# Subtract, square and sum over rows: coarser pieces for the last rows, and ScalarE as the engine that waits for the store

## The chip, the cores and the metric

The kernel runs on one core of a Trainium2 chip. The metric is the device time of one execution in microseconds (us). The engines that matter here are VectorE (DVE in the profile), ScalarE (ACT), and SyncE (SP), which issues every DMA. TensorE does nothing, and GpSimd (POOL) only sets a few constants at the start.

## The reference

```python
"x": np.random.randn(1024, 4096).astype(np.float32)
"y": np.random.randn(1024, 4096).astype(np.float32)
"axis": -1
...
return np.sum((x - y) ** 2, axis=axis).astype(np.float32)
```

Two matrices of 16.8 MB each are read once; 1024 sums of 4096 squared differences come out.

## The kernel before

**Layout.** Each of the 128 partitions holds 8 consecutive rows of the matrix, so that x and y are views of 128 partitions by 32768 columns (`N`), in which row r of a partition takes the columns 4096 r to 4096 r + 4095 (L56 to L62). The on-chip buffers X and Y have room for 24576 columns (`H`, six rows) each; a column c lies at c modulo H, so the columns of rows 6 and 7 go where those of rows 0 and 1 were (`home`, L98).

**Loads.** The lists `xw` and `yw` (L72, L73) cut the columns into loads: x in 7, y in 8 and two more. Those two are `last` (the last 192 columns of row 7) and `late` (the last 128 columns of row 3, which are held back and loaded at the very end). A load of y comes after the x that it needs. Two loads (x0, y0) are put ahead of the program's opening barriers by `early` (L29), x1 and y1 follow, and they fill the buffers. The other thirteen wait on SP until ScalarE has squared row 1 (L221) and are then issued one after the other (L108). All of them go through one DMA queue, SP's, and are served in that order. In short the loads are named here by their place in the lists: x2 is the third load of x, y2 the third of y, and so on.

**Work.** The loop at L197 goes over the loads of y. VectorE waits for the load (`wait_loaded`, L164), and for each piece of it (`pieces_of`, L128: cut at the ends of rows, and, for loads 1 to 4 of y, each part cut once more in half) it subtracts Y from X in place (`sub`, L176). ScalarE waits for that subtraction and squares the piece in place (`square`, L182); an accumulator read after each square writes the sum of the piece to a column of `parts`, or straight to `results` if the row is one piece. `complete` (L187) has VectorE wait for the last square of a row and add up the row's columns (L189). After load 4 of y VectorE completes rows 4, 5 and 6; row 7 at the end. The late piece is the exception: VectorE itself squares and sums it in one instruction (L205) on top of the partial sum of row 3.

**End.** SP waits until every reduction is done, issues the store of the results (L233), clears the semaphores of the program, and waits for the store's semaphore `stored` to reach 16, from which it takes 16 off again (`close`, L40 to L45).

**Pieces of the last four rows.** Row 4 and row 5 are two pieces of 2048 columns each; row 6 is 1312, 1312, 736 and 736; row 7 is 640, 672, 672, 672, 480, 480, 288 and 192. So ScalarE makes 16 squares for the rows 4 to 7.

Of the kernel before, what the change touches and what calls it, by code (L numbers as in the profile page):

```python
# [8 lines left out]
class Program:  # L9
# [27 lines left out]
        )  # L37
        self.entry[where:where] = taken

    def close(self, engine, stored, value):  # L40

        engine.sem_clear(range(self.sems[0].num, self.sems[-1].num + 1))
        engine.wait_ge(stored, value).then_inc(stored, -value)  # L45


def kernel(tc, x, y, axis, out):
    nc = tc.nc
    P = nc.NUM_PARTITIONS  # L50
    F32 = mybir.dt.float32
    Square = mybir.ActivationFunctionType.Square
    mult, add = mybir.AluOpType.mult, mybir.AluOpType.add

    B, D = x.shape
    R = B // P  # L56
    N = R * D


    xv = x.rearrange("(p r) d -> p (r d)", p=P)  # L60
    yv = y.rearrange("(p r) d -> p (r d)", p=P)
    ov = out.rearrange("(p r) -> p r", p=P)  # L62


    H = 6 * D
    X = nc.alloc_sbuf_tensor("X", [P, H], F32).ap()
    Y = nc.alloc_sbuf_tensor("Y", [P, H], F32).ap()
    results = nc.alloc_sbuf_tensor("results", [P, R], F32).ap()

    xw = [16384, 8192, 5472, 1280, 960, 320, 160]  # L72
    yw = [16256, 8192, 2624, 2784, 1344, 480, 480, 288]  # L73
    late, last = 128, 192
    LATE = 3
    halved = (1, 2, 3, 4)
    cut = (LATE + 1) * D - late
    assert sum(xw) == N and sum(yw) == N - late - last
    xs, c = [], 0
    for w in xw:  # L80
        xs.append((c, c + w))
        c += w
    ys, c = [], 0
    for w in yw:
        ys.append((c, c + w))
        c += w
        if c == cut:
            c += late
    ys += [(N - last, N), (cut, cut + late)]

    prog = Program(nc, tc)
    stored = nc.alloc_semaphore("stored")
    diffs = prog.semaphore("diffs")
    acts = prog.semaphore("acts")
    sums = prog.semaphore("sums")
    n = dict(diffs=0, acts=0, sums=0)

    def home(c0, c1):  # L98
        h0 = c0 % H
        return slice(h0, h0 + c1 - c0)  # L100


    landed_x, landed_y = [], []
    freed = []

    def load(landed, src, dst, name, c0, c1):
        sem = prog.semaphore("%s%d" % (name, len(landed)))
        nc.sync.dma_start(out=dst[:, home(c0, c1)], in_=src[:, c0:c1]).then_inc(sem, 16)  # L108
        landed.append(((c0, c1), sem))

    order = []
    have = 0
    for c0, c1 in ys:
        while have < c1:
            order.append((landed_x, xv, X, "x") + xs[len([o for o in order if o[3] == "x"])])
            have = order[-1][5]
        order.append((landed_y, yv, Y, "y", c0, c1))

    todo = list(order)
    for _ in range(2):  # L120
        load(*todo.pop(0))
    prog.early(mybir.EngineType.SP)
    while todo and todo[0][5] <= H:
        load(*todo.pop(0))


    row_parts = [[] for _ in range(R)]
    def pieces_of(j, c0, c1):  # L128

        pieces = []  # L130
        while c0 < c1:
            e = min(c1, (c0 // D + 1) * D)
            if j in halved:
                h = (c0 + e) // 64 * 32
                pieces.append((c0, h))
                c0 = h
            pieces.append((c0, e))
            c0 = e
        return pieces

    for j, (c0, c1) in enumerate(ys):
        for piece in pieces_of(j, c0, c1):
            row_parts[piece[0] // D].append(piece)
    parts, where = None, {}
    total = sum(len(p) for p in row_parts if len(p) > 1)
    parts = nc.alloc_sbuf_tensor("parts", [P, total], F32).ap()
    k = 0
    for r, p in enumerate(row_parts):
        for piece in p:
            where[piece] = parts[:, k : k + 1] if len(p) > 1 else results[:, r : r + 1]  # L150
            k += len(p) > 1
    first = {}
    k = 0
    for r, p in enumerate(row_parts):
        if len(p) > 1:
            first[r] = k
            k += len(p)

    def parts_of(r, m):
        return parts[:, first[r] : first[r] + m]  # L160

    seen_x = [0]

    def wait_loaded(c1, ysem):  # L164

        waits = []
        while seen_x[0] < len(xs) and xs[seen_x[0]][0] < c1:
            waits.append(seen_x[0])
            seen_x[0] += 1
        nc.vector.wait_ge(ysem, 16)  # L170
        for k in waits:
            nc.vector.wait_ge(landed_x[k][1], 16)

    def sub(c0, c1):
        a = X[:, home(c0, c1)]
        nc.vector.tensor_sub(out=a, in0=a, in1=Y[:, home(c0, c1)]).then_inc(diffs, 1)  # L176
        n["diffs"] += 1

    def square(c0, c1, acc):
        a = X[:, home(c0, c1)]  # L180
        nc.scalar.wait_ge(diffs, n["diffs"])
        nc.scalar.activation(out=a, in_=a, func=Square, accum_out=acc).then_inc(acts, 1)  # L182
        n["acts"] += 1

    squared = {}

    def complete(r):  # L187
        nc.vector.wait_ge(acts, squared[row_parts[r][-1]])
        nc.vector.tensor_reduce(  # L189
            out=results[:, r : r + 1],  # L190
            in_=parts_of(r, len(row_parts[r])),
            axis=mybir.AxisListType.X,
            op=add,
        ).then_inc(sums, 1)
        n["sums"] += 1

    for j, (c0, c1) in enumerate(ys):  # L197
        final = j == len(ys) - 1
        wait_loaded(c1, landed_y[j][1])
        for piece in pieces_of(j, c0, c1):  # L200
            sub(*piece)
            r = piece[0] // D
            if final:
                nc.vector.wait_ge(diffs, n["diffs"])
                nc.vector.tensor_tensor_reduce(  # L205
                    out=Y[:, home(*piece)],
                    in0=X[:, home(*piece)],
                    in1=X[:, home(*piece)],
                    scale=1.0,
                    scalar=parts_of(r, 1),  # L210
                    op0=mult,
                    op1=add,
                    accum_out=results[:, r : r + 1],
                ).then_inc(sums, 1)
                n["sums"] += 1
                continue
            square(*piece, where[piece])
            squared[piece] = n["acts"]
            if r in (0, 1):

                nc.sync.wait_ge(acts, n["acts"])  # L221
                while todo and todo[0][5] <= H + (r + 1) * D:
                    load(*todo.pop(0))
                if r == 1:
                    while todo:
                        load(*todo.pop(0))
        if j == 4:
            for r in (4, 5, 6):
                complete(r)
    complete(7)  # L230

    nc.sync.wait_ge(sums, n["sums"])
    nc.sync.dma_start(out=ov, in_=results).then_inc(stored, 16)  # L233
    prog.close(nc.sync, stored, 16)


# [33 lines left out]
```

## Time and profile before

| what | value |
|---|---|
| time, median of 3 runs | 84.24 us (84.09 to 84.29) |
| the profiled execution: its time | 84.24 us |
| the profiled execution: its span, first to last instruction | 82.9 us |
| DVE busy | 36.9 us (44%), 27 instructions |
| ACT busy | 33.5 us (40%), 41 instructions |
| DMA queue, share of the 16 engines' span | 95.8%, 33.56 MB, mean 405 GB/s |
| subtractions (L176) | 21, 36.3 us |
| squares (L182) | 20, 31.2 us |

The span is 1.34 us shorter than the time: what lies before the first and after the last instruction isn't in the trace. A busy row of the page has one digit for each fortieth of the span, in tenths of that slice. The chain of waits lists, in order of time, what the end of the program was waiting for. In the timeline a line is a start, a length, the engine, the line of the kernel, and the tiles; in brackets is the idle time before it and what ended it. A row of the groups has the shape, the count, the busy time, the mean length in ns of one instruction, and the idle time before. A row of the DMA issues has the kilobytes and the time from the issue to the landing in us. SPq is the sequencer of SP, whose issues, waits and clears are not counted as busy.

### The profile page before, as it was taken

To read this page: it belongs to the slowest core of one execution; us is meant where nothing else is said; L and a number is where in the kernel's file an instruction comes from. 1 tells how busy PE (TensorE), PEld (TensorE's weight loads), DVE (VectorE), ACT (ScalarE), POOL (GpSimd) and SP (SyncE) were. 2 spreads that over 40 slices of the span, in tenths; PEclk is the share of its full clock that TensorE was granted. 3 is DMA by queue.
4 is the path that set the end of the run, shared out by engine and by line. 5 is a ranking of instruction groups with operands and counts; after the bars stand their busy time and mean duration, and the time that the engine had idled before them with its cause. 6 is when DMAs were issued, how large, how long until landed. Compare 5 with 4: busy or idle time off the path is not lost.

```text
span 82.9 us, 135 instructions
## 1 busy us (share of the span) xinstructions
DVE 36.9 (44%) x27; ACT 33.5 (40%) x41; POOL 0.2 (0%) x4
## 2 busy tenths in 40 slices
DVE  0000000000000000000299999999189996989992
ACT  0500000000000000000000979889886999899991
POOL 0000000000000000000000000000000000000000
DMA  9299999957999996599799979969989899999960
GB/s 506 95 411 506 506 506 506 474 221 316 502 502 502 502 502 282 220 502 502 316 443 506 427 332 506 490 269 506 411 348 496 369 405 438 430 403 421 396 214 2
DMA packets 2592, 33.56 MB, mean 405 GB/s; under 512 B 416, under 2 KB 1312, under 8 KB 1696
## 3 DMA queue, kind: packets, MB, share of 16 engines
q1 hardware_dynamic: 2592, 33.56, 95.8%
HBM read 33.55 MB, written 0.00 MB: 405 GB/s over the span
## 4 chain that ended last, share of the span: by engine, by line
DMA 64%; SPq 17%; DVE 12%; ACT 4%; issue 1%
DMA Y<-in_y_dram 64%; SPq L108 17%; DVE X L176 11%; ACT X L182 4%; DVE Y L205 0%; DVE results L189 0%; SPq L221 0%; DVE results L205 0%
## 5 line engine op out<-in xcount | busy, mean ns | idle before, releaser
L176 DVE TENSOR_TENSOR X<-X,Y 128x2048 f32<-128x2048 f32 (+10 forms) x21 | 36.3, 1779 | 44.5 <-DMA Y<-in_y_dram 44.4
L182 ACT ACTIVATE X<-X 128x2048 f32<-128x2048 f32 (+9 forms) x20 | 31.2, 1559 | 45.9 <-DVE X L176 45.8
L182 ACT ACTIVATION_READ_ACCUMULATOR X<-X 128x1 f32 x20 | 3.7, 186 | 0.0
L182 ACT ACT_TABLE_LOAD x1 | 1.3, 1283 | 1.9 <-PEq L19 1.9
L189 DVE TENSOR_REDUCE results<-parts 128x1 f32<-128x2 f32 (+2 forms) x4 | 0.4, 151 | 0.0
L205 DVE CUSTOM_DVE_ANT_0 Y<-X,parts 128x128 f32<-128x128 f32 x1 | 0.4, 353 | 0.0
L251 POOL MEMSET const-bfloat16-1.0<- 128x1 bf16 x1 | 0.1, 101 | 0.0
L251 POOL MEMSET const-uint8-127<- 128x1 uint8 x1 | 0.1, 101 | 0.0
L251 POOL MEMSET const-float32-0.0<- 128x1 f32 x1 | 0.1, 98 | 0.2 <-issue 0.2
L251 POOL MEMSET const-float32-1.0<- 128x1 f32 x1 | 0.1, 98 | 0.0
L205 DVE DVE_READ_ACCUMULATOR2_ANT results<- 128x1 f32 x1 | 0.1, 84 | 0.0
## 6 DMA issues: line engine op xcount, KB each, us to landing
Y<-in_y_dram SPq DMA_DIRECT2D x1, 8128.0 KB, 40.6
X<-in_x_dram SPq DMA_DIRECT2D x1, 4096.0 KB, 48.8
Y<-in_y_dram SPq DMA_DIRECT2D x1, 4096.0 KB, 58.2
X<-in_x_dram SPq DMA_DIRECT2D x1, 2736.0 KB, 13.4
Y<-in_y_dram SPq DMA_DIRECT2D x1, 1392.0 KB, 19.0
Y<-in_y_dram SPq DMA_DIRECT2D x1, 1312.0 KB, 16.2
Y<-in_y_dram SPq DMA_DIRECT2D x1, 672.0 KB, 21.2
X<-in_x_dram SPq DMA_DIRECT2D x1, 640.0 KB, 20.1
```

The source lines that it names most:

```text
L108: nc.sync.dma_start(out=dst[:, home(c0, c1)], in_=src[:, c0:c1]).then_inc(sem, 16)
L176: nc.vector.tensor_sub(out=a, in0=a, in1=Y[:, home(c0, c1)]).then_inc(diffs, 1)
L182: nc.scalar.activation(out=a, in_=a, func=Square, accum_out=acc).then_inc(acts, 1)
L189: nc.vector.tensor_reduce(out=results[:, r : r + 1], in_=parts_of(r, len(row_parts[r])), axis=mybir.AxisListType.X, op=add,).then_inc(sums, 1)
L205: nc.vector.tensor_tensor_reduce(out=Y[:, home(*piece)], in0=X[:, home(*piece)], in1=X[:, home(*piece)], scale=1.0, scalar=parts_of(r, 1), ...
L251: nc = _bacc.Bacc("TRN2", target_bir_lowering=False, num_devices=1)
```

## The change

Three things are edited.

- The loads after the first two are cut otherwise: x in 6, y in 7 and the two at the end, which now have 288 columns (`last`) and 160 (`late`). That makes 15 loads in place of 17. The first y load loses 32 columns, which the late piece gains.
- The halving in `pieces_of` is gone. Rows 4 and 5 are one piece each (4096), whose sums go straight to `results`; row 6 is 2656 and 1440; row 7 is 1472, 928, 896, 512 and 288. ScalarE makes 9 squares for the rows 4 to 7. Only row 6 is completed after load 4 of y.
- In `close`, ScalarE waits for the store and takes the 16 off; SP still clears the other semaphores.

```diff
-    def close(self, engine, stored, value):
+    def close(self, engine, last, stored, value):
         engine.sem_clear(range(self.sems[0].num, self.sems[-1].num + 1))
-        engine.wait_ge(stored, value).then_inc(stored, -value)
+        last.wait_ge(stored, value).then_inc(stored, -value)
...
-    xw = [16384, 8192, 5472, 1280, 960, 320, 160]
-    yw = [16256, 8192, 2624, 2784, 1344, 480, 480, 288]
-    late, last = 128, 192
+    xw = [16384, 8192, 5568, 1824, 512, 288]
+    yw = [16224, 8192, 2656, 2912, 928, 896, 512]
+    late, last = 160, 288
     LATE = 3
-    halved = (1, 2, 3, 4)
...
-    def pieces_of(j, c0, c1):
+    def pieces_of(c0, c1):
         pieces = []
         while c0 < c1:
             e = min(c1, (c0 // D + 1) * D)
-            if j in halved:
-                h = (c0 + e) // 64 * 32
-                pieces.append((c0, h))
-                c0 = h
             pieces.append((c0, e))
             c0 = e
         return pieces
...
         if j == 4:
-            for r in (4, 5, 6):
+            for r in (6,):
                 complete(r)
     complete(7)
...
-    prog.close(nc.sync, stored, 16)
+    prog.close(nc.sync, nc.scalar, stored, 16)
```

More of the change, by code (lines that the diff above doesn't have):

```diff
@@ L139, in pieces_of @@
         return pieces
-    for j, (c0, c1) in enumerate(ys):
-        for piece in pieces_of(j, c0, c1):
+    for c0, c1 in ys:
+        for piece in pieces_of(c0, c1):
             row_parts[piece[0] // D].append(piece)
@@ L199 @@
         wait_loaded(c1, landed_y[j][1])
-        for piece in pieces_of(j, c0, c1):
+        for piece in pieces_of(c0, c1):
             sub(*piece)
```

## The prediction, on record before the changed kernel ran

> **What bounds the kernel now.** I read the page first. Its busy shares (DVE 44%, ACT 40%, DMA queue 95.8%) are averages over a span of which the first 41 us only load, so the 40 slices (2.07 us each) say more.
>
> ```profile
> DVE  0000000000000000000299999999189996989992
> ACT  0500000000000000000000979889886999899991
> DMA  9299999957999996599799979969989899999960
> ```
>
> The loads run without a hole until slice 38. In the last ten slices VectorE (DVE) and ScalarE (ACT) are nearly full too: three resources run out almost together, and the end must be read from the chain of waits (start, length, what; us).
>
> ```profile
> 67.69 12.66 DMA Y<-in_y_dram
> ...
> 80.37 0.57 DVE X L176 x2
> ...
> 80.96 0.35 DVE Y L205
> 81.32 0.01 DVE results L205
> 81.33 0.11 DVE results L189
> ```
>
> The last-but-one y load lands at 80.34; VectorE then needs two subtractions (192 and 128 columns), the fused square of the late piece (L205) and the reduction of row 7 (L189). SP issues the store at 81.47. But that reduction also waits for ScalarE's last square; the timeline shows how close that is.
>
> ```profile
> 69.45 1.91 ACT L182 ACTIVATE X<-X 128x2048 f32<-128x2048 f32 x1 [0.20 <-DVE X L176]
> ...
> 71.76 1.30 ACT L182 ACTIVATE X<-X 128x1312 f32<-128x1312 f32 x1 [0.31 <-DVE X L176]
> ...
> 80.81 0.34 ACT L182 ACTIVATE X<-X 128x192 f32<-128x192 f32 x1
> ...
> 81.06 0.18 ACT L182 ACTIVATION_READ_ACCUMULATOR X<-X 128x1 f32 x1
> ...
> 81.28 0.16 DVE L189 TENSOR_REDUCE results<-parts 128x1 f32<-128x8 f32 x1
> ```
>
> ScalarE delivers at 81.06 + 0.18 = 81.24 and the reduction starts at 81.28. Other ScalarE and VectorE instructions also start 0.03 us after the one they wait for, so ScalarE has no slack: whatever delays it delays the end.
>
> **The change part by part.** Durations of other widths come from the rows by shape (busy, mean ns).
>
> ```profile
> L176 DVE TENSOR_TENSOR X<-X,Y 128x4096 f32<-128x4096 f32 x3 | 13.1, 4421 | 41.0 <-DMA Y<-in_y_dram 41.0
> L176 DVE TENSOR_TENSOR X<-X,Y 128x2048 f32<-128x2048 f32 x4 | 8.9, 2286 | 2.2 <-DMA Y<-in_y_dram 2.2
> L182 ACT ACTIVATE X<-X 128x4096 f32<-128x4096 f32 x3 | 10.8, 3617 | 43.5 <-DVE X L176 43.5
> L182 ACT ACTIVATE X<-X 128x2048 f32<-128x2048 f32 x4 | 7.6, 1910 | 1.5 <-DVE X L176 1.5
> L182 ACT ACTIVATE X<-X 128x288 f32<-128x288 f32 x1 | 0.4, 426 | 0.0
> ```
>
> A subtraction is 0.15 us + 1.04 ns a column ((4421-2286)/2048), and the next starts 0.08 before it ends. A square is 0.20 us + 0.834 ns a column; its accumulator read ends 0.09 after it, and the next square doesn't wait for that.
>
> *Loads.* Thirteen loads follow the first four; the change has eleven. A landing is issue start (timeline) plus time to landing (DMA issues): y1 at 2.29 + 58.2 = 60.5, then
>
> ```profile
> X<-in_x_dram SPq DMA_DIRECT2D x1, 2736.0 KB, 13.4
> Y<-in_y_dram SPq DMA_DIRECT2D x1, 1392.0 KB, 19.0
> Y<-in_y_dram SPq DMA_DIRECT2D x1, 1312.0 KB, 16.2
> ```
>
> 53.63 + 13.4 = 67.03 for x2, 54.00 + 16.2 = 70.2 for y2, 54.48 + 19.0 = 73.5 for y3: 1.20 ns a column. Loads of 480 columns take about 1.3 ns a column and the last small ones 1.4 to 1.5, so a load itself costs some 0.04 to 0.08 us. Two fewer save 0.1 us, and 32 columns moved from y0 to the late piece bring y1 0.04 earlier. New landings: y1 60.46, x2 (5568) 67.11, y2 (2656) 70.30, y3 (2912) 73.78, x3 (1824) 75.96, y4 (928) 77.07, y5 (896) 78.15, x4 and y6 (512 each, 0.65) 79.45, x5 and last (288 each, 0.36) 80.17, late (160) 80.39, against 80.5 before. SP's issue instructions block for 2.6 to 4.8 us each near the end, but each load still lands 9.9 us or more after its issue began, so fewer issues gain nothing more.
> The Trainium skill's page "DMA: Bandwidth & Descriptors" (Anatomy of one DMA; Rules for kernel authors) gives a DMA a fixed cost of about 2.0 us, fitted on another issuing path, and says that transfers under 64 KB pay mostly overhead. Taken as a cost in this queue, two loads fewer would save 4 us and the time would be near 80.2, an estimate by that page; but thirteen times 2.0 is 26 us, more than the 20.0 us in which all thirteen land here. The row decides.
>
> *VectorE, rows 4 to 7.* Rows 4 and 5 become one subtraction each, from 60.48 to 60.48 + 4.34 + 4.42 = 69.24. The 2656 piece waits for y2: 70.32 + 2.92 = 73.24. Then 1440 (73.80 to 75.45), 1472 (to 77.06), 928 on its landing (77.10 to 78.22), one reduction in place of three, 896 (78.21 to 79.30), 512 on its landing (79.48 to 80.17), 288 on its landing (80.20 to 80.65), 160 (80.58 to 80.89), the fused square from 80.93. Before, the reduction started 0.32 after the fused square; 32 more columns make it 0.35: VectorE is ready at 81.28, as before. The earlier landing and the longer last pieces cancel.
>
> *ScalarE, rows 5 to 7.* Here the halves are missed. Row 5's square starts at 69.27 and frees ScalarE at 72.89. The 2656 square can't start before 73.24 + 0.03 = 73.27, where the first half started at 71.76 before. From there on the squares are back to back, each subtraction ending at or before its turn (1472 just in time, the others with 0.2 to 0.4 to spare): 2656, 1440, 1472, 928, 896, 512 and 288 columns take 2.42 + 1.40 + 1.43 + 0.97 + 0.95 + 0.63 + 0.43 = 8.23. So 73.27 + 8.23 = 81.50, accumulator read to 81.59, reduction at 81.62 in place of 81.28. **+0.34 us.** The check: the start is 1.51 later, five fewer squares at 0.20 give back 1.0, and the gaps of before (0.12) go. The wait is now ScalarE's, and VectorE idles 0.34 ahead of the last reduction.
>
> *Other reductions.* Those of rows 4 and 5 vanish and row 6's has two parts. It waits for the 1440 square, done at 77.2, and VectorE gets there at 78.15: no stall. If ScalarE were a microsecond later, VectorE would stand there with 896, 512, 288 and late queued behind it.
>
> *The closing wait.* SP keeps the store's issue and the clear of the semaphores; ScalarE waits for the store. Nothing is queued behind it in the program, and ScalarE's own work ends 1.6 us before the store lands.
>
> ```profile
> SPq L45 <- SPq L45: 1.0, 1, 1.0
> ```
>
> Inside the span this is a swap: at the three barriers at the start (L251, L19; semaphore records of the trace) SP and ACT wake from one release 4 to 5 ns apart, in the second at 1.503 and 1.508, and take 17 ns each. What follows the last instruction, part of the 84.24 - 82.90 = 1.34 us around the span, isn't in the trace. From below: if all that SP does after its last instruction now runs during the store, at most the 1.0 us that it waits there can be gained. From above: an extra hand-over among the engines, at most like a whole barrier at the start (SP's release in the first at 1.176, in the second at 1.503), +0.33. I take 0, by the nearest row, the 5 ns, and keep -1.0 and +0.33.
> The Trainium skill's page "Runtime: NRT & Kernel Launch" (The ~15µs preamble/postamble breakdown) names a barrier after the kernel that waits for all engines, and for the one before it a walk of 44 ns a hop over eight hops. Which engine is last could by that page move the end by a few hops, some 0.2 us either way as an estimate; no row here shows it.
>
> **The sum**, against the profiled execution, whose time of 84.24 is also the median: 84.24 + 0.34 (ScalarE) + 0 (closing) = **84.58 us**, span 83.24. About 0.3% (0.25 us) is what a measurement of this kernel can tell from no change.
>
> **The rivals.**
> - *Forecast*: ScalarE's late start, closing free: 84.58, with 0.1 us of doubt in the landing of y2, which the whole ScalarE chain follows. Chance 0.50.
> - *Closing costs* up to a barrier: 84.6 to 84.91. For: nothing in the trace covers what follows the last instruction. Against: 5 ns at the starting barriers. 0.10.
> - *The cost is smaller, or half covered*: y2 lands early (ScalarE can't start before 72.89, so 84.20 at best), or handing the end to ScalarE gains 0.1 to 0.6: 83.99 to 84.48. For: y2's stretch has only one row of evidence. 0.27.
> - *Faster, by the closing*: SP's own exit is the long part outside the span, and it now runs beside the store's 1.0 us. It must exceed 0.34 to beat before and 0.59 to show; at its full price 84.58 - 1.0 = 83.58. For: SP is idle from 81.93 to 82.89 and still has a queue to close; its drain after the first issues takes 125 ns where ACT's takes 8. Against: that is a fifth of what is needed. 0.13.
> - *The change doesn't do what it says* (the time outside is the same whoever waits) is the forecast itself.
>
> **Numbers.** Slower by over 0.3% (above 84.49): 0.50 + 0.10, less the doubt of y2 = 0.57. Same: 0.27 and that doubt = 0.30. Faster 0.13. The range goes from 83.99, which leaves out the last rival alone, to 84.91.
>
> **What would show it.** ScalarE without a gap from 73.3 to 81.5; the chain of waits ending through a square of 288 columns instead of the late piece; the last landing near 80.4; the store issued near 81.81. A first long square near 73.0 would mean that y2 was early. Closing shows as a change of the time outside the span, 1.34 now. A store at 81.47 or earlier would make the ScalarE step wrong; a time outside the span that moved by more than 0.1 would make the closing step wrong.

## The result and the profile after

The changed kernel takes 84.75 us (median of 4 runs, 84.69 to 84.88) against 84.27 us for the kernel before in the same comparison: a ratio of 1.0064, 95% interval 1.0044 to 1.0083. It is slower by 0.54 us (0.37 to 0.70). The forecast was 84.58 us and slower; the sign, the engine and more than half of the size came as forecast, one term didn't.

The profiled execution of the changed kernel takes 84.88 us with a span of 83.38 (before: 84.24 and 82.90). So the loss of this execution lies in two places: 0.48 us more inside the span, and 1.50 us around the span in place of 1.34.

The page of the changed kernel, busy shares in 40 slices of 2.08 us:

```profile
DVE  0000000000000000000299999999099994979981
ACT  0500000000000000000001979797970797989991
DMA  9299999957999999299989979997999999999940
```

In the 34th slice (68.8 to 70.9) VectorE waits for y2 and is 4 tenths busy (6 before); from the 37th on (75.1) ScalarE is hardly ever idle, and in the 39th (79.2 to 81.3), where the loads end, ScalarE is at 9 and VectorE at 8 (both 9 before). The chain of waits of the changed kernel (start, length, what) ends through ScalarE:

```profile
54.05 16.39 DMA Y<-in_y_dram
70.45 0.02 issue
70.47 2.94 DVE X L170
73.41 0.02 issue
73.43 8.29 ACT X L176 x14
81.72 0.02 issue
81.74 0.16 DVE results L183
```

Before, the chain ran from the last loads through VectorE. Now the load named is y2, which lands at 70.45, eleven microseconds before the end; one subtraction follows, and then seven squares with their accumulator reads (x14) with no gap over 0.02 us. A second chain ends almost level with this one. The load y3 brings 1440 and 1472 columns, and the second of its two subtractions ends at 75.53 + 1.69 = 77.22; the square of those 1472 columns starts 0.03 later, at 77.25, just as ScalarE comes free:

```profile
75.53 1.69 DVE L170 TENSOR_TENSOR X<-X,Y 128x1472 f32<-128x1472 f32 x1
75.85 1.39 ACT L176 ACTIVATE X<-X 128x1440 f32<-128x1440 f32 x1
77.25 1.43 ACT L176 ACTIVATE X<-X 128x1472 f32<-128x1472 f32 x1
```

So an earlier start of ScalarE's run would by itself not end it earlier; e10 below shows that. VectorE is the one that waits at the end, as the waits of the changed kernel say (us in total, times, longest):

```profile
DVE results L183 <- ACT X L176: 0.2, 1, 0.2
```

The timeline of the changed kernel shows both engines at the end:

```profile
80.57 0.62 ACT L176 ACTIVATE X<-X 128x512 f32<-128x512 f32 x1
...
81.14 0.38 DVE L199 CUSTOM_DVE_ANT_0 Y<-X,parts 128x160 f32<-128x160 f32 x1
81.18 0.43 ACT L176 ACTIVATE X<-X 128x288 f32<-128x288 f32 x1
81.45 0.08 DVE L199 DVE_READ_ACCUMULATOR2_ANT results<- 128x1 f32 x1
81.52 0.19 ACT L176 ACTIVATION_READ_ACCUMULATOR X<-X 128x1 f32 x1
81.74 0.16 DVE L183 TENSOR_REDUCE results<-parts 128x1 f32<-128x5 f32 x1 [0.21 <-ACT X L176]
81.92 0.35 SPq L227 DMA_DIRECT2D out_dram<-results  x1
```

The store is issued at 81.92 where it was 81.47. Nothing in the span is lost after that: the store lands 1.42 us after its issue (1.41 before).

### The profile page after: what moved, and what is told of

The parts are those of the page before. It is cut to its first block, busy times and chain, and to the rows that moved or that the text cites. A ratio compares the mean times of both kernels' runs of the same rounds, so it can differ in the third digit from the quotient of the medians.

```text
span 83.4 us, 109 instructions
## 1 busy us (share of the span) xinstructions
DVE 36.3 (44%) x18; ACT 31.7 (38%) x27; POOL 0.2 (0%) x4
## 4 chain that ended last, share of the span: by engine, by line
DMA 68%; ACT 14%; DVE 14%; SPq 1%; issue 0%
DMA Y<-in_y_dram 68%; ACT X L176 14%; DVE X L170 14%; SPq L107 1%; DVE results L183 0%; SPq L215 0%
## 5 line engine op out<-in xcount | busy, mean ns | idle before, releaser
L170 DVE TENSOR_TENSOR X<-X,Y 128x4096 f32<-128x4096 f32 (+9 forms) x14 | 35.8, 2593 | 45.3 <-DMA Y<-in_y_dram 45.2
L176 ACT ACTIVATE X<-X 128x4096 f32<-128x4096 f32 (+8 forms) x13 | 29.7, 2288 | 48.1 <-DVE X L170 48.1
L176 ACT ACTIVATION_READ_ACCUMULATOR X<-X 128x1 f32 x13 | 2.4, 187 | 0.0
```

## The experiments

Theory A when they began: 0.35 to 0.45 us of ScalarE's tail inside the span, and 0.15 us outside it because ScalarE is the last engine. Rival B: the closing wait is free. Rival C: the wider last pieces on VectorE set the end. "Around the span" is an execution's time less its span, averaged over the timed runs.

**e1: the closing wait alone.**

```diff
-        engine.wait_ge(stored, value).then_inc(stored, -value)
+        last.wait_ge(stored, value).then_inc(stored, -value)
...
-    prog.close(nc.sync, stored, 16)
+    prog.close(nc.sync, nc.scalar, stored, 16)
```

> The kernel before with only the closing wait moved to ScalarE; sizes and halves stay. Theory A (the change cost two things: some 0.35 to 0.45 us of ScalarE's tail inside the span, and 0.15 us outside it, because ScalarE is now the last engine: 84.88 - 83.4 = 1.5 around the span after, 1.34 before): 84.27 + 0.15 = 84.42 us, span still 82.9. Rival B (the closing is free, as predicted; the difference around the span is chance between two executions): 84.27 us.

Measured: 84.46 us against 84.24, ratio 1.0029 (1.0016 to 1.0041). The mean span of its 12 runs is 82.94, that of the kernel before 82.92 (23 runs); around the span it is 1.51 against 1.34. Rival B falls: the wait costs 0.17 us, all of it after the last instruction of the trace.

**e2: the change without the closing wait.**

```diff
-    prog.close(nc.sync, nc.scalar, stored, 16)
+    prog.close(nc.sync, nc.sync, stored, 16)
```

> The changed kernel with only the closing wait given back to SP. Theory A: 84.75 - 0.15 = 84.60 us, span still 83.2 to 83.4, so that the time around the span is 1.34 again. Rival B: 84.75 us.

Measured: 84.47 us, ratio to the kernel before 1.0029 (1.0018 to 1.0040), and 1.33 us around the span. So pieces and sizes together cost 0.24 us (0.15 to 0.34). Rival B falls; theory A's 84.60 is missed by 0.13; it started from the 84.75 us of only four executions. Its chain of waits is that of the changed kernel, 0.27 us earlier because y2 lands at 70.18:

```profile
70.18 0.02 issue
70.20 2.94 DVE X L170
73.14 0.02 issue
73.16 8.29 ACT X L176 x14
81.45 0.02 issue
81.48 0.16 DVE results L183
```

**e3: the halves alone taken out of the kernel before.**

```diff
-    halved = (1, 2, 3, 4)
+    halved = ()
...
-            for r in (4, 5, 6):
+            for r in (6,):
```

> The kernel before with only the halving taken out (row 6 alone is completed after load 4 of y); sizes and SP's closing wait stay. Theory A (ScalarE starts its last run of squares only when the whole piece of y2 is subtracted): 2624 columns are subtracted at 70.20 + 2.88 = 73.08, then eight squares back to back, 8192 x 0.834 ns + 8 x 0.20 = 8.46, to 81.57, reduction at 81.7 in place of 81.28: 84.27 + 0.4 = 84.67 us. Rival C (the loss comes from the wider last pieces of 288 and 160 columns, not from the halves): 84.27 us.

Measured: 84.68 us, ratio 1.0052 (1.0037 to 1.0068), so rival C falls. The chain of waits has the run that was worked out, eight squares from the end of one long subtraction, and the reduction at 81.64:

```profile
70.16 2.90 DVE X L176
73.07 0.02 issue
73.09 8.53 ACT X L182 x16
81.62 0.02 issue
81.64 0.16 DVE results L189
```

**e4: the sizes alone, halves kept.**

```diff
-    xw = [16384, 8192, 5472, 1280, 960, 320, 160]
-    yw = [16256, 8192, 2624, 2784, 1344, 480, 480, 288]
-    late, last = 128, 192
+    xw = [16384, 8192, 5568, 1824, 512, 288]
+    yw = [16224, 8192, 2656, 2912, 928, 896, 512]
+    late, last = 160, 288
```

> The kernel before with only the sizes of the loads changed (6 of x, 9 of y, 288 and 160 columns at the end); the halves of loads 1 to 4 and SP's closing wait stay. Theory A: ScalarE starts on the first half of y2 near 71.9, eleven squares take 6.83 + 2.23 = 9.06, so it is never the last by more than 0.1 us, and the end follows the last loads: 84.25 to 84.45 us. Rival C (the wider last pieces are the loss): 84.6 us or more.

Measured: 84.59 us, ratio 1.0047 (1.0031 to 1.0062). Theory A missed this: the sizes cost 0.35 us though loads 1 to 4 keep their halves. The price is rival C's, the place isn't, as the timeline of e4 shows:

```profile
78.29 2.49 DVE L176 TENSOR_TENSOR X<-X,Y 128x896 f32<-128x896 f32 x4
...
79.41 0.95 ACT L182 ACTIVATE X<-X 128x896 f32<-128x896 f32 x1 [0.26 <-DVE X L176]
...
80.35 0.61 ACT L182 ACTIVATE X<-X 128x512 f32<-128x512 f32 x1
80.81 0.39 DVE L205 CUSTOM_DVE_ANT_0 Y<-X,parts 128x160 f32<-128x160 f32 x1
...
80.97 0.43 ACT L182 ACTIVATE X<-X 128x288 f32<-128x288 f32 x1
81.12 0.08 DVE L205 DVE_READ_ACCUMULATOR2_ANT results<- 128x1 f32 x1
...
81.52 0.16 DVE L189 TENSOR_REDUCE results<-parts 128x1 f32<-128x7 f32 x1 [0.32 <-ACT X L182]
```

VectorE's fused square of 160 columns is done by 81.2, and VectorE then waits 0.32 for ScalarE. ScalarE had caught up with its work and stood for 0.26 us until the 896 columns of load 5, which `halved` doesn't name, were subtracted; then it had three wide squares in a row. In e4 a wide piece near the end delays ScalarE although the earlier ones are halved.

**e9: e4 with load 5 halved too**, the test of that step.

```diff
-    halved = (1, 2, 3, 4)
+    halved = (1, 2, 3, 4, 5)
```

> The run with the sizes alone changed lost 0.35 us, which theory A had not foreseen: its ScalarE waited until 79.41 for the subtraction of the 896 piece (load 5 of y, which is not halved) and then had 896, 512 and 288 columns to square in a row, so that the reduction started at 81.52. This kernel is that one with load 5 halved too (448 and 448). Theory A with this step added: the first 448 can be squared at 79.05, four squares take 0.57 + 0.57 + 0.61 + 0.43, reduction at 81.35: 84.59 - 0.17 = 84.42 us. Rival C (VectorE's wider last pieces of 288 and 160 set the end): no change, 84.59 us.

Measured: 84.34 us, ratio 1.0015 (1.0004 to 1.0027); e4 was at 1.0047 (1.0031 to 1.0062). The timeline of e9:

```profile
79.15 0.56 ACT L182 ACTIVATE X<-X 128x448 f32<-128x448 f32 x1
...
79.71 0.56 ACT L182 ACTIVATE X<-X 128x448 f32<-128x448 f32 x1
...
80.27 0.61 ACT L182 ACTIVATE X<-X 128x512 f32<-128x512 f32 x1
...
80.88 0.43 ACT L182 ACTIVATE X<-X 128x288 f32<-128x288 f32 x1
...
81.43 0.16 DVE L189 TENSOR_REDUCE results<-parts 128x1 f32<-128x8 f32 x1
```

ScalarE's wait is gone, and rival C falls, since VectorE's last pieces are as wide as in e4. One cut brings back 0.25 of the 0.35 us (0.17 expected; of the 0.08 between, no run here says whether it is chance). No run takes apart the 0.1 us that is left against the kernel before.

**e10: e2 with load 2 alone halved.** The kernel of e4 with this edit:

```diff
-    halved = (1, 2, 3, 4)
+    halved = (2,)
...
-            for r in (4, 5, 6):
+            for r in (6,):
```

> The sizes of the change with SP's closing wait and only load 2 of y halved (1312 and 1344). Theory A: ScalarE's run starts when row 5's square ends, 72.9, in place of 73.16 without halves, and has one more square of 0.20: reduction at 81.4 in place of 81.48, 84.47 - 0.07 = 84.40 us. Rival (the halving of load 2 alone is what the change lost): 84.24 us, as the kernel before.

Measured: 84.53 us, ratio 1.0035 (1.0021 to 1.0050), so neither the 0.07 us of theory A nor the rival's 0.24 is gained. The timeline of e10 shows what ate it:

```profile
73.00 1.28 ACT L182 ACTIVATE X<-X 128x1312 f32<-128x1312 f32 x1
...
74.27 1.31 ACT L182 ACTIVATE X<-X 128x1344 f32<-128x1344 f32 x1
...
75.44 1.68 DVE L176 TENSOR_TENSOR X<-X,Y 128x1472 f32<-128x1472 f32 x1
75.58 1.39 ACT L182 ACTIVATE X<-X 128x1440 f32<-128x1440 f32 x1
...
77.16 1.43 ACT L182 ACTIVATE X<-X 128x1472 f32<-128x1472 f32 x1
```

ScalarE starts at 73.00 but ends the 1440 square at 76.97 and gets the whole 1472 piece only at 77.16: the run is broken at the next uncut piece, whose subtraction ends at 77.12. That piece follows the landing of y3: from there to its square it is 3.32 us in the changed kernel, in e2 and in e10 (landings at 73.93, 73.67 and 73.84), and to the last reduction 7.81 us in all three.

**e8: the kernel before with rows 4 and 5 whole**, all other halves kept.

```diff
-    halved = (1, 2, 3, 4)
+    halved = (2, 3, 4)
...
-            for r in (4, 5, 6):
+            for r in (6,):
```

> The kernel before with the halves of load 1 of y alone taken out: rows 4 and 5 are one piece each and need no reduction; loads 2 to 4 keep their halves. Theory A (ScalarE's run of squares is back to back from its start, so its start and its number of squares give the end): row 5's subtraction ends at 69.27, its square at 72.9, and the twelve squares left take 8192 x 0.834 ns + 12 x 0.20 = 9.27, to 82.2, reduction at 82.3 in place of 81.28: 84.24 + 1.0 = 85.25 us, slower than with no halves at all (84.68). Rival (each load's halves save their share, so that fewer halves lose less): between 84.24 and 84.68 us.

Measured: 85.13 us, ratio 1.0110 (1.0095 to 1.0125). The chain of waits of e8:

```profile
69.48 12.77 ACT X L182 x26
82.25 0.02 issue
82.27 0.16 DVE results L189
```

Thirteen squares without a gap from the end of row 5's subtraction, and the reduction at 82.27 where 82.3 was worked out. Here fewer halves are worse than none (e3, 84.68): row 5, squared whole, frees ScalarE only at 73.09, and the small pieces behind it keep their 0.20 us each.

**e5, e6, e7: another engine closes the kernel before.** The edit of e1 with `nc.vector`, `nc.gpsimd` and `nc.tensor`.

> The kernel before with only the closing wait given to VectorE. So far the time outside the span is 1.34 us when SP is last (23 executions) and 1.51 us when ScalarE is (12). Theory A1 (what follows the last instruction goes through the engines one after the other, so its length depends on which engine comes last): a third value between 1.2 and 1.6 us, other than both. Rival A2 (SP is the exception, any other engine as the last costs the same): 1.51 us around the span, 84.41 us in all. Span 82.9 in both.

> The kernel before with only the closing wait given to GpSimd, which has nothing else to do after its first constants. Theory A1: a value between 1.2 and 1.6 us around the span, other than VectorE's and ScalarE's. Rival A2: 1.51 us around the span, 84.41 us in all. Span 82.9 in both.

> The kernel before with only the closing wait given to TensorE, which does nothing else. Theory A1: a value between 1.2 and 1.6 us around the span; if the engines are gone through in a fixed order, the five values lie some 0.04 to 0.08 us apart from one engine to the next, the size of the hand-overs in the barriers at the start of the trace. Rival A2: 1.51 us around the span, 84.41 us in all. Span 82.9 in both.

| last engine | time, us | ratio to before (95%) | mean span, us | around the span, us (runs) |
|---|---|---|---|---|
| SP (before) | 84.24 | | 82.92 | 1.34 (23) |
| VectorE | 84.31 | 1.0019 (1.0005 to 1.0032) | 82.91 | 1.45 (10) |
| ScalarE (e1) | 84.46 | 1.0029 (1.0016 to 1.0041) | 82.94 | 1.51 (12) |
| TensorE | 84.60 | 1.0040 (1.0026 to 1.0053) | 82.88 | 1.67 (5) |
| GpSimd | 84.80 | 1.0071 (1.0052 to 1.0089) | 82.93 | 1.87 (4) |

The ratios for VectorE, TensorE and GpSimd are to 14 runs of the kernel before in their own comparison (84.22 us, 1.34 us around the span). In each group the times around the span scatter by 0.03 to 0.04 (one standard deviation), which the rounding of the recorded spans to 0.1 us explains by itself, so these are five values. Rival A2 (SP alone is the exception) falls. TensorE and GpSimd also lie outside the 1.2 to 1.6 that theory A1 allowed. The spans are alike, and the wait itself is short everywhere, 17 to 51 ns, as the row of the closing line in GpSimd's run shows:

```profile
L45 POOLq EVENT_SEMAPHORE  x1: 17/17/17, 83.0 to 83.0; - x1
```

Theory A1 is right in kind and wrong in its sizes, as the trace itself shows. Its views stop at the last instruction, but its semaphore records, from which the prediction read the barriers at the start, go on. A semaphore that isn't one of the kernel's (number 2) is updated nine times just ahead of the first instruction, and at the end of the program nine times and then nine times again. The first nine at the end begin while the program still runs, and they stop until the engine that closes is done (times in us from the end of the last instruction):

| last engine | of the nine, done before the closing wait ended | next one at | ninth at | last of the second nine at |
|---|---|---|---|---|
| SP (before) | 4 | 0.14 | 0.31 | 1.45 |
| VectorE | 3 | 0.19 | 0.43 | 1.57 |
| ScalarE (e1) | 1 | 0.15 | 0.47 | 1.62 |
| TensorE | 0 | 0.28 | 0.63 | 1.78 |
| GpSimd | 2 | 0.56 | 0.85 | 1.99 |

The counts give a fixed order of turns: TensorE first, then ScalarE, GpSimd, VectorE and SP, and after SP's turn four more updates. From the ninth to the last of all it is 1.14 to 1.15 us whoever closes, so the whole difference lies ahead of the ninth: 0.12, 0.17, 0.33 and 0.54 us above SP's, as the times around the span say (0.11, 0.17, 0.33, 0.53). It has two parts, how long the closing engine takes to its turn and how many turns are left. ScalarE reaches its turn as soon as SP does (0.15 and 0.14), but has seven steps behind it in place of four, 0.32 us in place of 0.16. GpSimd loses 0.42 us on the way to its turn.

## Why the prediction was right, and where it wasn't

**ScalarE's tail: right in its mechanism, a little too large.** The run of squares was forecast from 73.27 to 81.50, with the reduction at 81.62. The changed kernel has 73.43 and 81.74, e2 has 73.16 and 81.48, and each follows its own landing of y2 (70.45 and 70.18, forecast 70.30): from the landing to the reduction it is 11.29 and 11.30 us, forecast 11.32. "1472 just in time" came true to 0.02 us; the prediction didn't say that this is a second chain, from y3, of the same length. Over many runs the term is e2's 0.24 us (0.15 to 0.34) against the forecast 0.34. The profiled execution of the changed kernel, taken alone, would say 0.46; its y2 lands 0.27 later than e2's. The prediction's check of the term, 1.51 - 1.0 - 0.12, comes to 0.39 and not to 0.34.

**"Here the halves are missed": true only in the sizes of before.** The prediction worked out the run of squares correctly and then put the loss on the missing halves. With SP closing, the four combinations are:

| | sizes of before | sizes of the change |
|---|---|---|
| halves of loads 1 to 4 | 84.24 us | 84.59 us (e4) |
| no halves | 84.68 us (e3) | 84.47 us (e2) |

In the sizes of before the halves are worth 0.44 us. In the sizes of the change the halves of loads 1 to 4 are worth nothing (84.59 with, 84.47 without; the intervals of the ratios overlap), and those of load 2 alone nothing either (e10, 84.53). Either edit alone makes ScalarE the last, and the two don't add: without halves the run starts at much the same time in both sizes (73.09 in e3, 73.16 in e2), and the new sizes make it one square shorter (8.53 and 8.29 us). The prediction never asked what the new sizes do while the halves are there, where the uncut 896 columns of load 5 come late; e9 shows that step.

**The closing wait at 0: the step that failed.** The prediction took the 5 ns between SP and ACT at the starting barriers as its nearest row. That row tells of waking up, and waking up is indeed alike. The price lies after the last instruction: 0.17 us in e1, 0.16 in the changed kernel (1.50 on the mean of its four runs), more than the 0.1 that the prediction had named as the sign that this step is wrong. What the views don't show there, the semaphore records do, so "isn't in the trace", which stands in the prediction and ahead of it, and "no row here shows it" don't hold: in the changed kernel as in e1 the ninth update comes at 0.47 us, with SP last at 0.31. The two nines at the end of the trace of before are the nearer row: from ScalarE's turn to the end the second takes 0.32 us, from SP's turn to the end the first takes 0.16, and the difference is the 0.16 that was missed. The price lay within the bounds kept (-1.0 to +0.33), as the rival "closing costs", but this rival should have been likelier. With the measured terms the sum is 84.24 + 0.24 + 0.17 = 84.65, against 84.75 measured in another comparison, whose kernel before was 0.03 higher. That the forecast of 84.58 lies so near this sum is partly luck: a tail forecast 0.10 too large stood against a closing 0.17 too small. GpSimd's 0.53 us is more than the +0.33 that the prediction gave as the most for any hand-over.

The Trainium skill's page "Runtime: NRT & Kernel Launch" (The ~15µs preamble/postamble breakdown) names a barrier behind the kernel that waits for all engines, and gives eight hops of 44 ns for the walk of the one ahead of it. The traces here agree with both: the nine updates ahead of the kernel take 0.37 us from first to last in the trace of before, in eight steps of 0.02 to 0.11, and with TensorE, the first in the order, closing, those behind it take 0.36. The eight hops make 0.35 us in all by the page, less than the 0.53 us between the table's ends; 0.42 of these are GpSimd's own way to its turn.

**The loads: in agreement, but not shown.** The last landing was forecast at 80.39, 0.14 us before that of the kernel before (80.53), for two loads fewer and for y1 landing earlier. In the profiled executions with 13 late loads it lies at 80.52 on the mean (seven kernels, 80.41 to 80.63), with 11 at 80.40 (five kernels, 80.27 to 80.60). Kernels with the same loads scatter by more than the difference. And 0.08 of the 0.12 is there when y1 lands, before any late load: from y1's landing to the last it is 19.98 us with 13 loads and 19.94 with 11, which also move 32 columns more. Whatever was gained there was useless, since ScalarE was the last in all five kernels with 11 loads.

**The rival "faster by the closing": its condition was false.** SP leaving early gained nothing in any run.

No kernel tried is faster than the kernel before. What is left open is why GpSimd takes 0.56 us and TensorE 0.28 from the closing wait to their turns, where the other three take 0.14 to 0.19.

## What to carry to other kernels

When two engines work one behind the other on the last loads, write down the second one's run of work from the moment after which it has no gap any more: start, plus 0.20 us a piece, plus its columns. Then look for a second chain of the same length. Cutting a piece helped where the engine stood waiting for that piece (e9), and not where the next uncut piece came just as late (e10), so do this for each edit with the others in place and taken out. What the last engine is can be worth as much as a tail of small pieces; time it with one line changed, and compare time less span, which shows 0.1 us where the time itself scatters by 0.5.

## What the runs showed of the hardware that was not expected

The time around the span depends on which engine ends the program: 1.34 us with SP, 1.45 with VectorE, 1.51 with ScalarE, 1.67 with TensorE and 1.87 with GpSimd, with the same span of 82.9. The semaphore records show the walk behind it, in the order TensorE, ScalarE, GpSimd, VectorE, SP, which waits at the turn of the engine that ends last. And the spans of one kernel differ from execution to execution by up to 0.5 us (82.7 to 83.2 in 23 runs of the kernel before), with the last loads landing up to 0.3 us apart between profiles.
